# Transposed keys laid out by residue, and cached values loaded four rows to a partition, in a hybrid attention and GLA step

## The chip, the cores and the metric

One core of one Trainium2 chip runs the whole step. The metric is device time in microseconds (us), the median of three runs.

## What is computed

One layer of a hybrid decoder, for a prompt of 2048 positions and for eight samples of eight new positions each, which have 2048 cached keys and values per head. A normed input is projected; eight heads of 64 attend in three dilated windows, and the three results are mixed by their softmax denominators:

```python
DILATED = ((128, 1), (512, 4), (2048, 16))      # (window, dilation)
n_keys = window // dil + 1
...
s = jnp.einsum('brnqhd,brnkhd->brnqhk', qr, kk) * (hd ** -0.5)    # prompt: by residue modulo dil,
s = jnp.where(valid[None, None, :, :, None, :], s, -jnp.inf)      # blocks of 128 and the one before
...
idx = W + jnp.arange(T)[:, None] - dil * jnp.arange(n_keys)[None, :]   # sample: gathered from the cache
kg, vg = k_buf[:, idx], v_buf[:, idx]
```

Beside it a gated linear attention (GLA) of four heads runs in chunks. Both results are gated, concatenated, multiplied with `w_out` (1024 x 1024) and added to the input. Softmax sums over the keys of a window, so the order in which the keys of a block stand does not matter, as long as mask and values stand in the same order.

## The kernel before

Matrix products that need float32 accuracy are split into float16 parts: a projection of 128 rows is 8 x 3 matmuls, a score of 128 queries is two matmuls (the two orders of the key's high and low half). A cost-driven scheduler places the instructions on each engine; the Python code gives it generators that are woven in proportion to their steps. SP issues every DMA, in order. The stages, by first and last matmul in the trace:

- from 0 to 462 us, q, k and v are projected for 16 tiles of 128 rows (`project`, L1120). Each tile's keys and queries are stored in float16 to `kp_d` and `qp_d`, its values to `vp_d`, and come back transposed by DMA: `keys` (L838) fills `kk`, `queries` (L848) fills `qq`. `kk` holds, for each head, two groups of 512 positions (`m % 2`), each in the order of positions.
- from 113 to 625 us the branches 1 and 2 of the prompt's attention run between the projections. `unit(m, pp, br, x)` (L858) is 128 queries of four heads: for branch 1 the block x of 128 positions of group m, for branch 2 the residue x modulo 4 of group m. `attend` (L395) does it in four steps: `qk` (scores, L408, then minimum, mask and exp at L416 and L419), `tr` (transposes, L426, split into two float16 parts), `pv` (values, L441). The moving operand of L408 is a slice of `kk`: for branch 1 contiguous positions, for branch 2 every fourth position. The values of a unit are loaded 128 rows at a time (L883).
- on POOL and DVE the sample's scores against the cached keys run beside it (`sample_scores`, L985, `dot`, L978).
- branch 3 (L931) follows from 625 to 803 us, then the GLA with the projections g, vb and gb, to 1142 us.
- from 1142 us to the end, the output: `combine(t)` (L1501) loads the three branches and gates of tile t and mixes them, mostly on DVE and POOL; `turned` (L1447) transposes the mix (tm, L1453); `finish` (L1474) multiplies it with `w_out` in 48 matmuls of 512 columns (Y, L1488). The sample's attention is woven in: `sample_pair` (L1651) takes two samples at a time, four times. Its `values` (L1735) multiplies probabilities with cached values (L1737): four matmuls, each using 32 of the array's 128 columns. Each of the 13 blocks of cached values of a sample is a load of 128 rows x 512 numbers (256 KB, L1763), with 8 buffers. The last tile's output waits for the sample's attention and the sample's own output (Y_s).

```python
keys:    SP.dma_start_transpose(kk[:, :, m % 2, P * a : P * a + P], kp_d[r0 : r0 + P, :])
branch 2: of = lambda k: k[:, :, slice(x, 512, 4)]          # in scores, L906
values:  v = ssk.tile([P, 512], F32, ..., tag="sv", bufs=8)
         SP.dma_start(v[:], of(cv[2 * bp + bb]))
```

## Time and profile before

| | |
|---|---|
| three runs | 1419.62, 1424.39, 1426.09 us |
| median | 1424.39 us |
| span of the profiled execution | 1424.9 us |
| PE busy | 1285.0 us, 90% of the span |
| DVE, ACT, POOL busy | 1018.0, 843.7, 621.9 us |
| DMA | 281.57 MB on one queue, 67.1% of the time of 16 engines |
| HBM | 183.19 MB read, 75.24 MB written |

The profiled execution's span is the time from the first to the last instruction of the program; it lies 0.5 us above the median of the runs, inside their spread of 6.5 us, so nothing else has to be added to it. A row of the grouped view names source line, engine, operation, tiles and shape, count, then busy time, mean duration of one in ns, and idle time before them. A matmul's duration is the time through the array, longer than the time until the next one can start, which the timeline shows. PE is the matmul itself, PEld its weight load.

### The profile page before, as it was taken

Reading aid. Unit: us, or ns where it says so; the run is one execution under the profiler, and the core shown is the slowest. Engines: PE = TensorE matmul, PEld = TensorE weight load, DVE = VectorE, ACT = ScalarE, POOL = GpSimd, SP = SyncE. Lnnn points to the kernel's source line nnn. Section 1 sums busy time; section 2 is a strip of 40 time slices with the busy share of each in tenths; the row PEclk is TensorE's granted clock in tenths of the full one; section 3 lists DMA queues with packets and bytes.
Section 4 is the critical chain, followed back from the end, with each engine's and each line's share of the span. In section 5 each row is a group of like instructions: output and inputs, shape, how many; then the busy total and the mean of one; then the engine's idle time right before and its main releaser. Section 6 shows DMA issues by size and latency. Waiting matters only on the chain.

```text
span 1424.9 us, 26506 instructions
## 1 busy us (share of the span) xinstructions
PE 1285.0 (90%) x8942; PEld 743.6 (52%) x8942; DVE 1018.0 (71%) x2459; ACT 843.7 (59%) x2259; POOL 621.9 (44%) x564
## 2 busy tenths in 40 slices
PE   5989999889898898996889999889999989999997
PEld 2434555455455554664667666666555434444343
DVE  6797697789798967666775357898877797773222
ACT  6466787667377775875677665777876542221120
POOL 0144355566577455554421486556551264340000
PEclk9999999999999899997999999999999999999998
DMA  8469756678966797888976444242235759998661
GB/s 297 156 188 255 192 161 150 182 203 215 240 165 173 208 288 239 260 217 228 234 190 179 149 123 116 87 153 91 88 119 176 267 179 344 359 316 267 221 215 63
DMA packets 246874, 283.27 MB, mean 199 GB/s; under 512 B 117889, under 2 KB 148690, under 8 KB 246738
## 3 DMA queue, kind: packets, MB, share of 16 engines
q1 hardware_dynamic: 246738, 281.57, 67.1%
q8 instruction: 71, 1.16, 0.4%
q14 instruction: 65, 0.53, 0.1%
HBM read 183.19 MB, written 75.24 MB: 181 GB/s over the span
## 4 chain that ended last, share of the span: by engine, by line
PE 35%; DVE 25%; DMA 16%; ACT 11%; issue 7%; POOL 4%; SPq 2%; DVEq 0%; POOLq 0%; ACTq 0%
PE Y L1488 7%; PE acc_g L1120 3%; PE acc_vb L1120 3%; PE acc_k L1120 3%; DMA k<-in_cache_k_win 2%; POOL pr L980 2%; PE s L408 2%; PE OS L1737 2%; PE acc_qkb L1120 2%; ACT p L419 2%; DMA o_d<-o 2%; DMA oc<-o_d 2%; DVE p L416 2%; PE acc_v L1120 2%; DMA T_q<-qp_d 2%
## 5 line engine op out<-in xcount | busy, mean ns | idle before, releaser
L980 POOL TENSOR_TENSOR pr<-k,qb 128x512 f32<-128x512 f32 x128 | 171.8, 1342 | 184.9 <-DVE sck L981 113.9
L1120 PEld LDWEIGHTS <-hr 128*128 128x128 f16 x1824 | 177.7, 100 | 138.2 <-issue 17.6
L419 ACT ACTIVATE p<-p,o 128x256 f32<-128x256 f32 (+1 forms) x384 | 173.1, 453 | 86.0 <-DVE o L416 83.3
L1120 PEld LDWEIGHTS <-hl 128*128 128x128 f16 x1248 | 123.2, 100 | 146.6 <-issue 22.2
L1488 PE MATMUL Y<-w_o,mh 128*128 128x512 f16 x768 | 182.9, 385 | 8.3 <-ACT mh L1454 4.9
L416 DVE CUSTOM_DVE_ANT_0 p<-s,m3w,scl_s 128x256 f32<-128x256 f32 (+1 forms) x384 | 143.6, 419 | 39.0 <-DMA o_d<-o 20.3
L393 POOL TENSOR_TENSOR pt<-p,pt 128x512 f16<-128x512 f32 (+1 forms) x80 | 98.3, 1229 | 139.6 <-ACT pt L392 107.3
L441 PE MATMUL O<-v,pt 128*128 128x128 f16 x1200 | 116.1, 224 | 25.3 <-POOL pt L393 10.0
L426 PE MATMUL t<-ident,p 128*128 128x128 f32 x600 | 119.0, 289 | 14.5 <-ACT p L419 9.2
L1488 PEld LDWEIGHTS <-mh 128*128 128x128 f16 x768 | 72.5, 99 | 103.7 <-issue 25.2
L408 PE MATMUL s<-kk,qq 128*128 128x256 f16 (+1 forms) x512 | 105.7, 326 | 17.5 <-DVE o L416 12.4
L981 DVE TENSOR_REDUCE sck<-pr 128x8 f32<-128x512 f32 x128 | 87.0, 680 | 44.0 <-POOL pr L980 43.7
L441 PEld LDWEIGHTS <-pt 128*128 128x128 f16 x1200 | 86.6, 101 | 54.6 <-POOL pt L393 13.6
L1120 PE MATMUL acc_g<-w_g,hr 128*128 128x272 f16 (+1 forms) x768 | 103.3, 285 | 1.9 <-DVE so_g L677 1.0
L1120 PE MATMUL acc_v<-w_v,hl 128*128 128x512 f16 x384 | 99.5, 405 | 4.6 <-DMA hl<-ht 3.7
L426 PEld LDWEIGHTS t<-ident,p 128*128 128x128 f32 x600 | 73.5, 146 | 43.2 <-ACT p L419 26.4
L1120 PE MATMUL acc_q<-w_q,hl 128*128 128x512 f16 x384 | 92.0, 380 | 1.9 <-ACT zs_q L703 1.4
L1120 PE MATMUL acc_k<-w_k,hl 128*128 128x512 f16 x384 | 91.3, 382 | 2.5 <-ACT w_k L658 1.3
L1454 ACT ACTIVATE mh<-tm 128x1024 f16<-128x1024 f16 x32 | 31.7, 1019 | 104.1 <-PE tm L1453 97.7
L1120 PE MATMUL acc_gb<-w_gb,hr 128*128 128x512 f16 x384 | 90.0, 388 | 2.1 <-DVE so_gb L677 2.1
L1120 PE MATMUL acc_vb<-w_vb,hr 128*128 128x512 f16 x384 | 89.3, 379 | 1.6 <-DVE so_g L677 1.6
L212 ACT ACTIVATE E<-D_e 128x256 f32<-128x256 f32 (+1 forms) x168 | 67.7, 411 | 27.1 <-DVE ks L219 17.6
(533 smaller groups left out, 2628.1 us busy)
## 6 DMA issues: line engine op xcount, KB each, us to landing
k<-in_cache_k_win SPq DMA_DIRECT2D x104, 256.0 KB, 4.3
sv<-in_cache_v_win SPq DMA_DIRECT2D x104, 256.0 KB, 5.4
hr<-h_d SPq DMA_DIRECT2D x44, 512.0 KB, 4.1
qb<-q_d SPq DMA_DIRECT2D x64, 256.0 KB, 4.6
oc<-o_d SPq DMA_DIRECT2D x48, 264.0 KB, 5.8
o_d<-o SPq DMA_DIRECT2D x64, 132.0 KB, 3.9
x<-in_x_prompt SPq DMA_DIRECT2D x16, 512.0 KB, 5.8
h_d<-hl SPq DMA_DIRECT2D x16, 512.0 KB, 4.7
```

The source lines that it names most:

```text
L212: ACT.activation(E[rows, i, :n], D[rows, half], AF.Exp, scale=1.0 / 16.0)
L393: POOL.tensor_tensor(l, f, h, ALU.subtract)
L408: PE.matmul(s_ps[:, i * w : (i + 1) * w], q, k, start=(n == 0), stop=(n == len(prods) - 1),)
L416: DVE.tensor_tensor_reduce(s[:, sl], s_ps[:, sl], mask, neg, BIG, ALU.add, ALU.min, nmf(i))
L419: ACT.activation(s[:, sl], s[:, sl], AF.Exp, bias=nmf(i), scale=-1.0, accum_out=denf(i))
L426: PE.transpose(p_ps[:, i * P : (i + 1) * P], t["s"][:, i * P : (i + 1) * P], ident[:])
L441: PE.matmul(o_, t["pt"][:, c, (i * nb + b) * P : (i * nb + b + 1) * P], vf(i, b), start=(n == 0), stop=(n == 2 * nb - 1),)
L980: POOL.tensor_tensor(pr[:], kt, qt, ALU.mult)
L981: DVE.tensor_reduce(out, pr[:].rearrange("p (u k d) -> p u k d", u=2, k=4), AX.X, ALU.add)
L1120: PE.matmul(z, a_[:, k, :], w[:, p_, k, cols], start=(k == 0 and i == 0), stop=(k == KT - 1 and i == 2),)
L1454: ACT.activation(mhl[:, a], pt[:], AF.Copy)
L1488: PE.matmul(Y[:], a_[:, k, :], w_[:, part, k, :512], start=(i == 0), stop=(i == len(prods) - 1),)
```

## The change

It does four things.

1. `kk` holds each group of 512 positions by residue modulo 4: four runs of 128, each for one residue. A transposing DMA now takes 128 rows that stand four apart in `kp_d`. Branch 2 reads one contiguous run of 128 (or 256 over two groups). Branch 1 reads, for each block of 128 positions, four runs of 32 positions (64 bytes) out of the four residues; its keys stand in the order of residue, so it has a mask of its own (`m1w`), and its values are loaded in that order (`by4`).
2. The sample's cached values are loaded in four pieces instead of 13: one of 256 KB, and three of 1 MB in which a partition takes four neighbouring rows (8 KB). Buffers: six of 1 MB, two of 256 KB. A generator step multiplies sixteen matmuls (four rows x four quarters of the array) after a piece.
3. The sample's attention is announced to the weaving with 4 x 9 steps instead of 4 x 16.
4. Constants (`ident64`, `m3w`, `tabs`) move to pools with a shorter life, and `ident8` is gone.

```diff
+    def by4(ap):
+        return ap.rearrange("(c r) f -> r c f", r=4)
...
         def keys(m, a):
-            r0 = 512 * m + P * a
-            SP.dma_start_transpose(kk[:, :, m % 2, P * a : P * a + P], kp_d[r0 : r0 + P, :])
+            SP.dma_start_transpose(
+                kk[:, :, a, m % 2, :], by4(kp_d[512 * m : 512 * m + 512, :])[a]
+            )
...
-                SP.dma_start(vt[:], sel(vp_d[:, pp * 512 : (pp + 1) * 512]))
+                rows = sel(vp_d[:, pp * 512 : (pp + 1) * 512])
+                SP.dma_start(vt[:], by4(rows) if br == 1 else rows)
...
                 def scores(i, a=a):
+                    k = kk[:, 4 * pp + 2 * a + i]
+                    q = [qs_[m, pp][:, order_, 2 * a + i] for order_ in range(2)]
                     if br == 2:
-                        qs = slice(x, 512, 4)
-                        of = lambda k: k[:, :, qs] if nb == 2 else k[:, m % 2, qs]
+                        k = k[:, x] if nb == 2 else k[:, x, m % 2]
+                        q = [f[:, x::4] for f in q]
                     else:
...
+                        n0 = 4 * (m % 2) + x
+                        if x or m % 2 or nb == 1:
+                            of = slice(n0 - nb + 1, n0 + 1)
                         else:
+                            of = slice(0, 8, 7)
+                        k = k.rearrange("p r s (b c) -> p r (s b) c", c=32)
+                        k = k.rearrange("p r b c -> p b r c")[:, of]
...
-        kk = ap_.tile([P, NH, 2, 512], F16, name="kk", tag="kk", bufs=1)
+        kk = ap_.tile([P, NH, 4, 2, P], F16, name="kk", tag="kk", bufs=1)
...
-            for c in range(4):
-                src.append((
-                    lambda x, c=c: p2[:, x, 32 * c : 32 * c + 32],
-                    lambda v, c=c: v[W - 512 : W, :].rearrange("(j r) c -> r j c", r=4)[c],
+            pieces.append((
+                "b2", [lambda x, c=c: p2[:, x, 32 * c : 32 * c + 32] for c in range(4)],
+                lambda v: v[W - 512 : W, :].rearrange("(j r) c -> j r c", r=4),
+            ))
+            for t0 in (0, 4):
+                pieces.append((
+                    f"b3{t0}",
+                    [lambda x, t=t: p3[:, x, 32 * t : 32 * t + 32] for t in range(t0, t0 + 4)],
+                    lambda v, t0=t0: v.rearrange("(m r) c -> m r c", r=16)[:, t0 : t0 + 4],
                 ))
...
-                    v = ssk.tile([P, 512], F32, name=f"sv_{bp}_{bb}_{i}", tag="sv", bufs=8)
+                    v = ssk.tile(
+                        [P, n, 512], F32, name=f"sv_{bp}_{bb}_{nm_}", tag=f"sv{n}",
+                        bufs=2 if n == 1 else 6,
+                    )
                     SP.dma_start(v[:], of(cv[2 * bp + bb]))
                     vs_.append(v)
-                held.append((ps, vs_, i + 1))
-                if i % 2 == 0:
-                    while held:
-                        values(*held.pop(0))
+                for j, p_ in enumerate(ps):
+                    step += 1
+                    values(p_, [v[:, j] for v in vs_], step)
+                if n > 1:
                     yield
...
-        weave(out, [sample_attention(), 4 * 16])
+        weave(out, [sample_attention(), 4 * 9])
```

More of the change, by code (lines that the diff above doesn't have):

```diff
@@ L105, in tile_hymba @@
     nw = const("nw", [P, KT], A["norm_w"][0].rearrange("(k p) -> p k", p=P))
-    ident8 = cp.tile([P, P], F32, name="ident8")
-    DVE.tensor_scalar(ident8[:], ident[:], 0.125, None, ALU.mult)
-    ident64 = cp.tile([P, 64], F32, name="ident64")
-    for r0 in (0, 64):
-        DVE.tensor_copy(ident64[r0 : r0 + 64], ident8[r0 : r0 + 64, r0 : r0 + 64])
     ident16 = cp.tile([P, P], F16, name="ident16")
@@ L373, in tile_hymba, with const1 @@
         vp = c_att.enter_context(tc.tile_pool(name="vp", bufs=11))
[L375 to L376 removed]
+        def const1(name, shape, src, dt=F32, pool=kp):
+            t = pool.tile(shape, dt, name=name, bufs=1)
             SP.dma_start(t[:], src)
@@ L1025, in tile_hymba @@
         gnw = const1("gnw", [P, P], A["gla_norm_w"].to_broadcast([P, P]))
-        m3w = const1("m3w", [P, 384], A["c_m3"])
+        m3w = const1("m3w", [P, 384], A["c_m3"], pool=ap_)
+        m1w = ap_.tile([P, 384], F32, name="m1w", bufs=1)
+        by_c, by_r = "p (b c r) -> p b r c", "p (b r c) -> p b r c"
+        DVE.tensor_scalar(
+            m1w.rearrange(by_r, r=4, c=32), m3w.rearrange(by_c, r=4, c=32),
+            1e-10, None, ALU.mult,
+        )
         DVE.tensor_scalar(m3w[:], m3w[:], 1e-10, None, ALU.mult)
-        masks12 = (m3w[:, 0:256], m3w[:, 128:384])
+        masks12 = [(w[:, 0:256], w[:, 128:384]) for w in (m1w, m3w)]
         m3 = m3w[:, 128:256]
-        tabs = kp.tile([P, 2, 2, 64], F32, name="tabs")
+        tabs = ap_.tile([P, 2, 2, 64], F32, name="tabs", bufs=1)
         scl = {n_: kp.tile([P, 1], F32, name=f"scl_{n_}") for n_ in "qks"}
@@ L1243, in tile_hymba @@
         Sbd = []
-        st = {"wgu": wgu, "E": [], "ks": [], "qbd": []}
+        ident64 = gst.tile([P, 64], F32, name="ident64")
+        for r0 in (0, 64):
+            DVE.tensor_scalar(
+                ident64[r0 : r0 + 64], ident[r0 : r0 + 64, r0 : r0 + 64], 0.125, None, ALU.mult
+            )
+        st = {"wgu": wgu, "ident64": ident64, "E": [], "ks": [], "qbd": []}
         for i in range(2):
```

37 lines of the change are left out of this document (13 added, 24 removed).

## The prediction

> **What bounds the kernel now.** I read the page's head first, then the busy time by window for the two stages that the change touches: the prompt's attention (113 to 625 us) and the output with the sample's attention (1166 us to the end).
>
> ```profile
> span 1424.9 us, 26506 instructions
> PE 1285.0 (90%) x8942; PEld 743.6 (52%) x8942; DVE 1018.0 (71%) x2459; ACT 843.7 (59%) x2259; POOL 621.9 (44%) x564
> ...
> core 0: us, PE busy (x) PEld busy (x) DVE busy (x) ACT busy (x) POOL busy (x), PEclk, DMA share, GB/s
> 113.00:625.00 512.00, 469.54 (x3096) 280.38 (x3095) 406.95 (x970) 358.03 (x1012) 287.86 (x218) 0.97 0.76 209
> 1166.00:1425.00 259.00, 241.70 (x1611) 107.33 (x1609) 127.80 (x263) 51.84 (x81) 55.20 (x44) 0.98 0.75 254
> 1170.00:1300.00 130.00, 123.35 (x846) 57.54 (x844) 91.88 (x192) 31.47 (x50) 51.51 (x40) 0.99 0.94 329
> ```
>
> PE is the busiest engine in both. The reader should see two more things: DVE is at 407 of 512 us in the first stage, and the DMA engines are at 0.94 in the first half of the second. Next I asked what the little PE idle time of the first stage (42 us) waits for, and whether SP is held in the second.
>
> ```profile
> PE s L408 <- DVE o L416: 12.4, 12, 2.3
> PE O L441 <- POOL pt L393: 8.1, 11, 2.4
> PE s L408 <- DMA kk<-kp_d: 5.0, 2, 3.9
> ...
> SPq L1763 <- PE OS L1737: 47.7, 23, 8.2
> ```
>
> So the attention's own chain (scores, minimum, exp, split, values) holds PE now and then; keys do so twice. In the output stage SP stood 47.7 us before loads of cached values until PE had given a buffer back.
>
> **Part 1, keys by residue.** A matmul's duration is its time through the array; what counts is the distance to the next start, from the timeline. Four score matmuls of branch 2, then four of branch 1, all with 256 columns:
>
> ```profile
> 274.30 1.08 PE L408 MATMUL s<-kk,qq 128*128 128x256 f16 x4
> 275.20 1.05 PE L1120 MATMUL acc_v<-w_v,hl 128*128 128x512 f16 x4
> ...
> 308.19 0.60 PE L408 MATMUL s<-kk,qq 128*128 128x256 f16 x4
> 308.63 3.62 PE L1120 MATMUL acc_v<-w_v,hl 128*128 128x512 f16 x16
> ```
>
> Branch 2 takes 0.90/4 = 0.225 us each, branch 1 0.44/4 = 0.110 us. The shape is the same; the difference is that branch 2's keys stand 8 bytes apart and branch 1's are contiguous. [...]
>
> What limits the contiguous read of branch 2 is next. Its queries are still read at a stride by the weight load, and the groups by shape show that load in a stretch of branch 2 (260 to 294 us) and of branch 1 (296 to 327 us), and the 128-column scores of branch 2 (145 to 174 us) beside those of branch 3:
>
> ```profile
> L408 PEld LDWEIGHTS <-qq 128*128 128x128 f16 x28 | 3.1, 118 | 3.1 <-issue 1.6
> L408 PEld LDWEIGHTS <-qq 128*128 128x128 f16 x28 | 2.6, 97 | 1.4 <-issue 0.7
> ...
> L408 PE MATMUL s<-kk,qq 128*128 128x128 f16 x31 | 5.2, 292 | 0.0
> L408 PE MATMUL s<-T_k,T_q 128*128 128x128 f16 x256 | 24.8, 231 | 0.3 <-DVE o L416 0.3
> ```
>
> If the strided weight load cannot be repeated faster than every 0.118 us, the 192 matmuls of 256 columns (three groups x 64) save 192 x (0.225 - 0.118) = 20.5 us, and the 64 of the first group little; if it hides altogether, 192 x 0.115 + 64 x 0.061 = 26 us. I take 22 us of PE time.
>
> Branch 1 pays for it: 240 matmuls now read runs of 64 bytes. No row has that. Its neighbours are 0.110 us for contiguous reads and 0.225 us for 2-byte pieces at 8 bytes, so the cost lies between 0 and 240 x 0.115 = 28 us. I take 0: a run of 32 elements is much nearer to the first. It cannot be below 0, because 0.110 is 256 columns at the rate of the 512-column matmuls (0.216, below).
>
> How much of the 22 us reaches the span? In the order of the built program the first scores stand behind 447 projection matmuls instead of 338: `keys` now needs all four tiles of a group, so its transposes queue on SP behind the last store of the group, with value loads behind them. PE does 109 projection matmuls first (109 x 0.216 = 24 us), which wait for nothing, so PE loses nothing there. But the attention's DVE work then has 24 us less room (407 in 488 us, 83%), and the waits quoted above do not shrink with PE's work. I let 60% through: 13 us, between 0 and 26. The strided transposes themselves are covered: branch 3 transposes rows 16 apart in the same way.
>
> Branch 1's values are loaded with four runs of 32 rows instead of 128 rows. The nearest row:
>
> ```profile
> v<-vp_d SPq DMA_DIRECT2D x64, 128.0 KB, 3.9
> ```
>
> PE never waits for it now, since four buffers let it go ahead. Bounds: 0, and 10 us for 32 loads if a third of a microsecond of each shows; I take 2. [...]
>
> **Part 2, sixteen matmuls at a time.** Values matmuls use 32 columns of the array each, four side by side. Each appears as two passes in the trace, so four matmuls are eight rows. The timeline around two broken quads, around a long block, and the plain rate of Y:
>
> ```profile
> 1306.83 0.39 PE L1488 MATMUL Y<-w_o,mh 128*128 128x512 f16 x1
> 1307.15 0.63 PE L1737 MATMUL OS<-sv,P3x 128*32 128x256 f32 x6
> 1307.71 4.49 PE L1488 MATMUL Y<-w_o,mh 128*128 128x512 f16 x20
> ...
> 1369.73 0.38 PE L1488 MATMUL Y<-w_o,mh 128*128 128x512 f16 x1
> 1370.04 0.64 PE L1737 MATMUL OS<-vs_t,Pn 64*32 64x256 f32 x8
> 1372.47 1.90 PE L1488 MATMUL Y<-w_o,mh 128*128 128x512 f16 x8
> ...
> 1411.72 8.80 PE L1488 MATMUL Y<-w_o,mh 128*128 128x512 f16 x40
> ```
>
> Y alone: (8.80 - 0.38)/39 = 0.216 us. Before a values block PE loses 0.32 - 0.216 = 0.10 us, and three quarters of a quad take 0.56 us, as much as a whole one: 0.66 us per block of at most one quad. Five quads take 2.43 + 0.10 = 2.53 us. So a block costs 0.20 us plus 0.465 us per quad, and a quad cut in two costs 1.31 us. In the built order of before, the 56 quads are cut into 61 blocks by single Y matmuls (56 blocks of at most a quad, one of 1.0 us, four of five quads): 56 x 0.66 + 1.0 + 4 x 2.53 = 48 us. In the changed order they stand in 10 blocks: 10 x 0.20 + 56 x 0.465 = 28 us. PE is relieved of 20 us.
>
> But the order also shows where the time may go. The last block of values stood beside tiles 14 and 15 (its last start is 1394.4 us); now all four pairs are done before Y of tile 8.
>
> ```profile
> L1737 PE MATMUL OS<-sv,P3x x256: 379/379/404, 1217.3 to 1394.4; 128*32 128x256 f32 x128
> L1763 SPq DMA_DIRECT2D sv<-in_cache_v_win x104: 327/382/1975, 1169.9 to 1387.2; - x104
> sv<-in_cache_v_win SPq DMA_DIRECT2D x104, 256.0 KB, 5.4
> ...
> 1230.00:1240.00 10.00, 10.00 (x69) 4.01 (x68) 8.51 (x13) 3.10 (x4) 6.85 (x5) 1.00 1.04 390
> 1270.00:1280.00 10.00, 9.48 (x90) 4.49 (x88) 8.04 (x14) 2.16 (x3) 6.93 (x7) 1.00 0.69 210
> 1410.16 10.37 PE Y L1488 x48
> L1453 PE MATMUL tm<-ident,mt 128*128 128x128 f16 x256 | 22.2, 220 | 1.4 <-ACT mh L1454 1.3
> ```
>
> From the first load of cached values to the last, SP's changed order holds 51.6 MB: the 27.3 MB of values, and the branches, gates and inputs that stand between. That is a wall in front of tile 8. At the stage's mean (329 GB/s) it takes 157 us, at the best ten microseconds (390) 132 us. I take 370, since fewer and longer loads should keep the queue filled: 139 us. The last load lands and is multiplied in 6 us. Behind it stand eight tiles (8 x 10.37 = 83 us), five tiles' transposes (80 x 22.2/256 = 7 us), the sample's output (32 x 0.216 = 7 us) and the tail from the last Y (1411.72 + 8.80 = 1420.5) to 1424.9, 4.4 us: 101 us. The first load starts at 1170 us on before's clock; I see nothing that moves it. So this stage ends at 1170 + 139 + 6 + 101 = 1416, 9 us earlier: less than half of PE's 20 us, because DMA bounds its first half and PE its second. By the two other rates it ends at 1409 and 1434, so the term lies between -16 and +9.
>
> **Parts 3 and 4** cost nothing by themselves: 4 x 9 steps is what makes the order above, and `ident64` and `m1w` are one or two DVE instructions, at GLA's start and 60 us ahead of the first mask.
>
> **Sum.** 1425 - 13 + 2 - 9 = 1405 us, against the profiled execution's own 1424.9 us, which is 0.5 us above the median of the runs, so the same number holds for the median.
>
> **Rivals.**
> - Both parts go through: the weight load hides, SP never stands still, 390 GB/s. 1425 - 26 - 16 = 1383 us. For it, PE at 92% in both stages; against it, DVE and DMA close behind. Chance 0.13.
> - The attention's chain replaces PE as the bound, and part 1 brings nothing: 1425 + 2 - 9 = 1418 us, around the line between faster and same. For it, the waits on L416 and L393 and the later start. Chance 0.16.
> - Slower, by one mechanism: SP stands before a load of cached values until PE has freed one of six 1 MB buffers, the branch loads behind it wait too, and the wall of 51.6 MB moves at 300 GB/s or less (single windows show 210, and the 47.7 us of SP's waiting show that it happens). At 300: 172 us, so 1170 + 172 + 6 + 101 - 11 = 1438 us. It decides below about 310 GB/s; against it, each 1 MB buffer holds what four did. Chance 0.14.
> - The wall at 329 GB/s takes part 1's gain back: 1434 - 11 = 1423 us. Chance 0.10.
> - Runs of 64 bytes cost half of their bound (14 us): 1419 us. Chance 0.04.
> - The change doesn't do what it says, because contiguous keys read no faster, the distance being set by the strided queries: 1418 us. Chance 0.03; the 0.118 us of the weight load speaks against it. [...]
>
> **How the numbers follow.** The forecast itself has 0.40. About 0.5% (7 us) is what a measurement of this kernel can tell from no change. Faster: 0.40 + 0.13, half of the three cases around 1418 (0.11) and a little of the 1423 case: 0.65. Slower: 0.15. Same: 0.20. The range reaches from 1380 (both parts in full) to 1436, leaving out most of the slower case; the forecast's own range is 1392 to 1418.
>
> **What would show it.** Right: 128x256 scores of branch 2 at 0.11 to 0.12 us in the timeline; values in rows of 32 or more, no single Y between them; PE waiting for DMA `sv` before tile 8 and for nothing after it; DMA near idle in the last 90 us. Wrong: scores of branch 1 above 0.12 us; the first stage as long as before though its PE time fell; last values landing later than 1330 us; a wait for `v` that was not there.

## The result, and the profile after

The changed kernel takes 1433.56 us (median; 1429.29 to 1435.01) beside 1425.16 us of the kernel before (six runs of each): ratio 1.0054, 95% interval 1.0033 to 1.0076. It is slower by half a per cent; 1405 us and "faster" had been forecast. The profiled execution took 1429.29 us; its span, 1427.5 us, is 1.8 us less. Every run's time lies some 2 us above its span, so the two are not the same measure. Ratios use fast runs alone; that leaves out one run, of 3892 us, of the kernel called *changed, spread* below.

First the page's head, and the busy time by window: the prompt's attention by the clock of before, the same stage by its own first and last score, and the output.

```profile
span 1427.5 us, 26392 instructions
PE 1253.2 (88%) x8942; PEld 746.4 (52%) x8942; DVE 1019.9 (71%) x2459; ACT 844.1 (59%) x2259; POOL 622.2 (44%) x564
```

```profile
113.00:625.00 512.00, 446.94 (x3031) 270.81 (x3028) 390.81 (x941) 348.83 (x981) 275.29 (x212) 0.96 0.76 206
137.00:638.00 501.00, 437.22 (x3031) 269.72 (x3031) 385.29 (x945) 346.63 (x987) 276.62 (x213) 0.96 0.75 204
1166.00:1425.00 259.00, 231.55 (x1647) 113.94 (x1644) 129.92 (x277) 54.34 (x85) 56.89 (x43) 0.95 0.69 257
1170.00:1300.00 130.00, 114.71 (x954) 57.97 (x951) 85.64 (x194) 34.70 (x58) 42.23 (x33) 0.92 0.98 373
```

PE was busy for 32 us less over the span (1285.0 to 1253.2), and the span grew by 2.6. In the stretch from 113 to 625 us PE works 22.6 us less, and DVE 16 us less too: less was done by 625 us (3031 matmuls for 3096), not the same in less time. Attention now runs from 137 to 638 us. In its own stretch PE sat idle for 512 - 469.5 = 42.5 us before and for 501 - 437.2 = 63.8 us now.

The timeline shows whether the read became cheap: four score matmuls of branch 2 (at 293.78, 256 columns), then four of branch 1 (at 322.31), each followed by the next group.

```profile
293.78 0.60 PE L405 MATMUL s<-kk,qq 128*128 128x256 f16 x4
294.22 0.94 PE L438 MATMUL O<-v,pt 128*128 128x128 f16 x14
...
322.31 0.60 PE L405 MATMUL s<-kk,qq 128*128 128x256 f16 x4
322.75 2.97 PE L1126 MATMUL acc_k<-w_k,hl 128*128 128x512 f16 x13
```

In the first group of positions branch 2 has 128 columns. Such scores before, then after:

```profile
151.52 1.10 PE L408 MATMUL s<-kk,qq 128*128 128x128 f16 x8
152.45 4.50 PE L1120 MATMUL acc_v<-w_v,hl 128*128 128x512 f16 x20
```

```profile
160.13 0.39 PE L405 MATMUL s<-kk,qq 128*128 128x128 f16 x4
160.36 0.59 PE L1126 MATMUL acc_v<-w_v,hl 128*128 128x512 f16 x2
```

The groups by shape give the weight loads of these scores (count, busy time and mean ns of one, idle time before), and the waits tell PE's idle time from 137 to 640 us (total, times, longest):

```profile
L405 PEld LDWEIGHTS <-qq 128*128 128x128 f16 x380 | 40.1, 109 | 24.3 <-issue 17.0
```

```profile
PE s L405 <- DVE o L413: 14.1, 11, 3.2
PE O L438 <- POOL pt L390: 13.7, 17, 1.9
PE O L438 <- DVE pt L386: 12.9, 9, 4.2
PE t L423 <- ACT p L416: 8.1, 9, 3.9
PE s L405 <- DMA kk<-kp_d: 3.7, 2, 3.3
```

The same two waits for DVE's part of the split and for exp before (113 to 625 us):

```profile
PE O L441 <- DVE pt L389: 5.2, 6, 2.2
PE t L426 <- ACT p L419: 1.5, 5, 0.3
```

ACT's wait for the row minima, before and after, in the same two windows:

```profile
ACT p L419 <- DVE o L416: 66.9, 46, 4.6
```

```profile
ACT p L416 <- DVE o L413: 94.9, 55, 5.1
```

Both branches take 0.44/4 = 0.11 us for a matmul: branch 2 fell from 0.225 us, branch 1 with its runs of 64 bytes pays nothing. The 128-column scores fell from 0.93/8 = 0.116 us to 0.23/4 = 0.058, so the weight loads keep up there too: their mean of 0.109 us is the time that one takes, not the distance between two. But PE waits 13.7 us for POOL's part of the split where it waited 8.1, and 12.9 us for DVE's where it waited 5.2.

In the output stage the values now stand in long blocks, as the timeline shows for the last pair; then the loads of the cached values (shortest, median and longest issue, first and last start), the stretch between those starts by window, and the last 90 us:

```profile
1311.57 0.64 PE L1748 MATMUL OS<-sv_w,P 128*32 128x256 f32 x8
1312.02 1.91 PE L1748 MATMUL OS<-sv_b,P2x 128*32 128x256 f32 x32
1313.75 3.64 PE L1748 MATMUL OS<-sv_b,P3x 128*32 128x256 f32 x64
```

```profile
L1779 SPq DMA_DIRECT2D sv_b<-in_cache_v_win x24: 327/348/709, 1175.0 to 1301.6; - x24
L1779 SPq DMA_DIRECT2D sv_w<-in_cache_v_win x8: 332/379/1020, 1173.8 to 1285.3; - x8
```

```profile
1173.80:1301.60 127.80, 115.54 (x956) 58.52 (x957) 83.40 (x189) 33.01 (x56) 40.59 (x32) 0.93 0.99 378
1330.00:1420.00 90.00, 88.82 (x475) 42.44 (x474) 20.99 (x28) 15.33 (x17) 0.51 (x1) 1.00 0.26 90
```

The wall was there, and after 1330 us DMA is at 0.26, as foreseen. It moved at 378 GB/s, where 370 had been taken.

The prediction did not look at one thing in these rows, the granted clock (PEclk). In the traces of before and of the changed kernel it stands at 1.00 or at 0.50, with stretches at 0.50 of 3.4 to 20.5 us. Thirteen matmuls of Y in the changed kernel at 0.50, then 31 at 1.00:

```profile
1322.50:1329.00 6.50, 5.46 (x13) 1.87 (x13) 5.01 (x13) 0.22 (x1) 2.55 (x2) 0.50 0.34 113
1331.00:1337.50 6.50, 6.50 (x31) 2.91 (x30) 1.41 (x2) 0.60 (x1) 0.00 (x0) 1.00 0.20 74
```

They take 0.42 us each, then 0.21. The mean granted clock was 0.951 to 0.957 in the six runs of the changed kernel, and 0.964 to 0.976 in all runs of the kernel before beside which the experiments were measured. What makes it drop, no run separates.

### The profile page after: what moved, and what is told of

Same layout as the page of the kernel before. It is cut to its first block, busy times and chain, and to the rows that moved or that the text cites. A ratio compares the mean times of both kernels' runs of the same rounds, so it can differ in the third digit from the quotient of the medians.

```text
span 1427.5 us, 26392 instructions
## 1 busy us (share of the span) xinstructions
PE 1253.2 (88%) x8942; PEld 746.4 (52%) x8942; DVE 1019.9 (71%) x2459; ACT 844.1 (59%) x2259; POOL 622.2 (44%) x564
## 4 chain that ended last, share of the span: by engine, by line
DVE 29%; PE 25%; DMA 16%; issue 13%; ACT 10%; POOL 6%; SPq 2%; POOLq 0%; DVEq 0%; ACTq 0%
PE Y L1499 6%; DVE p L413 3%; DMA k<-in_cache_k_win 3%; POOL pr L980 3%; DMA o_d<-o 3%; PE acc_vb L1126 2%; PE acc_g L1126 2%; DMA oc<-o_d 2%; PE acc_v L1126 2%; ACT p L416 2%; PE acc_k L1126 2%; DVE qbd L217 2%; PE acc_qkb L1126 1%; PE s L405 1%; DMA T_q<-qp_d 1%
## 5 line engine op out<-in xcount | busy, mean ns | idle before, releaser
L1499 PE MATMUL Y<-w_o,mh 128*128 128x512 f16 x768 | 177.6, 390 | 12.8 <-DVE xr L1506 9.4
L390 POOL TENSOR_TENSOR pt<-p,pt 128x512 f16<-128x512 f32 (+1 forms) x80 | 93.1, 1164 | 134.7 <-ACT pt L389 103.1
L413 DVE CUSTOM_DVE_ANT_0 p<-s,m3w,scl_s 128x128 f32<-128x128 f32 (+1 forms) x256 | 88.5, 395 | 28.5 <-DMA o_d<-o 24.5
L405 PE MATMUL s<-kk,qq 128*128 128x256 f16 (+1 forms) x512 | 80.9, 279 | 18.2 <-DVE o L413 14.1
L1126 PE MATMUL acc_vb<-w_vb,hr 128*128 128x512 f16 x384 | 90.6, 379 | 0.8 <-DVE so_g L674 0.8
L1547 POOL TENSOR_TENSOR tc<-oc,w 128x512 f32<-128x512 f32 x32 | 46.2, 1464 | 91.5 <-DVE w L1539 90.2
```

Of the source, the lines that this page charges most:

```text
L390: POOL.tensor_tensor(l, f, h, ALU.subtract)
L405: PE.matmul(s_ps[:, i * w : (i + 1) * w], q, k, start=(n == 0), stop=(n == len(prods) - 1),)
L413: DVE.tensor_tensor_reduce(s[:, sl], s_ps[:, sl], mask, neg, BIG, ALU.add, ALU.min, nmf(i))
L1126: PE.matmul(z, a_[:, k, :], w[:, p_, k, cols], start=(k == 0 and i == 0), stop=(k == KT - 1 and i == 2),)
L1499: PE.matmul(Y[:], a_[:, k, :], w_[:, part, k, :512], start=(i == 0), stop=(i == len(prods) - 1),)
L1547: eng.tensor_tensor(t_[:], oc[:, g, :, 0:64], w[:, g].unsqueeze(2).to_broadcast([P, NH, HD]), ALU.mult,)
```

## The experiments

The stages of every kernel are read from its trace by the same marks, in us: first score of the prompt, last score of branches 1 and 2, last score of branch 3, last matmul of projection g, first and last Y. The ratio is to the kernel before. The last three columns are of PE up to branch 3's last score: busy, idle, and how much of the busy time fell into half clock; half of that is counted as lost (0.42 us for 0.21, above). By then every kernel has run nearly the same matmuls (4639 to 4693, in the two with another rate 4603 and 4563). Before itself is in two rows, since single profiled executions of one and the same prompt part differ by a few us: "before", "constants" and the two values kernels have one order on PE there, and so have "changed", "changed, spread" and "layout only", of which the first and the last stand 6.7 us apart at branch 3's end.

```
                         first s  last s  last s(3)  last g  first Y  last Y   ratio      busy   idle   half
before                     113.0   624.9    787.1     992.6   1148.2   1420.1   1        696.3   90.8   52.6
constants only             112.1   622.6    784.3     989.6   1143.3   1419.1   1.0002   693.5   90.8   43.7
changed                    137.3   638.4    797.2    1001.1   1156.0   1422.7   1.0054   682.2  115.0   69.5
values only                112.8   624.4    785.2     990.5   1146.6   1408.2   0.9938   697.1   88.1   55.0
layout only                140.4   643.7    803.9    1006.1   1161.2   1439.4   1.0146   680.3  123.6   65.0
late keys                  131.9   616.9    777.8    1014.2   1145.8   1421.2   1.0062   687.1   90.7   48.4
cheap read                 110.1   606.6    775.1     966.8   1136.2   1410.2   0.9944   675.9   99.2   51.8
cheap read, late keys      132.7   605.6    767.1     969.7   1126.1   1389.9   0.9779   663.7  103.3   37.5
four tiles                 136.1   604.6    765.6     978.7   1122.4   1405.2   0.9925   670.6   95.0   51.7
four tiles, late           136.8   618.2    784.9     997.7   1152.4   1424.5   1.0075   671.8  113.1   49.1
four tiles, group 0 late   136.4   622.1    785.2    1008.7   1153.5   1418.8   1.0002   678.1  107.2   64.3
changed, values in order   137.9   621.6    794.0     996.5   1160.7   1426.9   1.0030   681.6  112.4   57.7
  and natural key loads    137.6   620.3    788.5    1001.4   1158.5   1422.5   1.0018   670.6  117.9   51.3
changed, keys first        138.1   631.1    796.5    1006.4   1161.8   1426.1   1.0085   675.6  120.9   50.0
changed, early group 0     112.0   632.8    788.3     989.6   1148.7   1413.8   0.9965   679.7  108.6   72.2
changed, spread            139.4   640.8    800.2    1004.0   1159.4   1411.8   0.9993   685.4  114.8   75.2
changed, both repairs      110.7   631.6    785.7     987.0   1142.5   1398.7   0.9891   676.5  109.1   62.3
values and spread          113.3   625.4    785.4     990.8   1146.1   1398.3   0.9858   692.9   92.5   43.9
rate 0.70, before          111.5   615.7    787.7    1030.0   1162.1   1436.8   1.0092   681.1  106.6   43.9
rate 0.70, changed         139.5   621.4    784.7    1034.0   1171.2   1432.3   1.0103   659.4  125.3   50.8
```

**Which part costs.** Four kernels of one chip. The theory: attention starts late and loses that time; the values part gains.

*Constants only* (`ident64`, `m3w` and `tabs` as in the change, nothing else).

> The kernel before with only the constants moved (ident64 made in the gated stage, the mask and the rotary tables in another pool). TensorE's order is the one of before. Every theory: no change, 1425 us within 4, first prompt score at 113 us within 2. Anything beyond that would say that pool places alone move the time by as much as the whole change did.

Measured 1421.88 us beside 1422.44: 1.0002 (0.9985 to 1.0019). Part 4 costs nothing that can be measured.

*Values only* (the constants, and parts 2 to 4 of the diff, on the layout of before).

> The kernel before with the constants moved and the new values loads and blocks of the sample, without the residue layout of the keys. Theory L (the late start of attention costs the time, the values part gains): the prompt stage as before, first score at 113 us, the output stage shorter by what it gained in the changed kernel, 5 us: 1420 us (1415 to 1423). Rival W (the output stage gains nothing by itself and only took up what came late): 1425 within 3.

1414.67 us, 0.9938 (0.9920 to 0.9957): 8.8 us less by the ratio, where 5 had been expected.

*Layout only* (the changed kernel with `src` and `held` of the old values part).

> The changed kernel with the old values loads and blocks of the sample, so the residue layout alone. Theory L: first score at 137 us, the end of branch 3 some 9 us later than before (812 against 803), and with the old output stage all of that at the end: 1434 to 1439 us, slower than the changed kernel. Rival D (the prompt stage loses nothing by itself, the changed kernel's loss sits in the output stage's wall of loads): 1420 to 1427.

1442.09 us, 1.0146 (1.0117 to 1.0175), 20.8 us more by the ratio. The whole loss is in the key layout; 0.9938 x 1.0146 = 1.0083, a little above the changed kernel's 1.0054.

Where it is lost can be read from the kernels that share an order up to branch 3's last score, four with the old prompt part and three with the changed one. On average PE is busy for 695.0 us and idle for 90.6 in the four, busy for 682.6 and idle for 117.8 in the three: 12 us less busy, 27 us more waiting, 15 us later. And of the busy time 49 us fall into half clock in the four and 70 in the three, which takes back some 10 us of what the cheap read saves. The rows of constants only and of the changed kernel:

```profile
0.00:784.30 784.30, 693.46 (x4676) 419.20 (x4677) 604.11 (x1573) 534.26 (x1528) 366.72 (x296) 0.97 0.76 210
```

```profile
0.00:797.20 797.20, 682.19 (x4681) 418.48 (x4682) 602.15 (x1575) 536.72 (x1529) 360.69 (x296) 0.95 0.75 207
```

*Late keys* (the layout of before):

```diff
-    for a in range(4):
-        keys(m, a)
+    with tc.issue_after(stored["k", 4 * m + 3].ins):   # the group's last store to kp_d
+        for a in range(4):
+            keys(m, a)
```

> The kernel before with its own layout of the keys, but the four transposed key loads of a group queued behind the store of the group's last key tile; the first score stands behind 496 projection matmuls instead of 410 (519 in the changed kernel). No read becomes cheaper. Theory L: attention starts some 20 us later and all of that but a few us is lost: first score 130 to 137 us, branch 3's end 815 to 825, 1436 to 1447 us. Rival (attention has room to catch up, and the changed kernel lost its time elsewhere, in the order of the loads or in the waits of the values): 1423 to 1430 in spite of a start as late.

1431.21 us, 1.0062 (1.0038 to 1.0085). The time lies between the two ranges, and the stages speak against theory L: attention started 20 us late and branch 3's last score still came 6.5 us earlier than with early keys (777.8, 784.3), with PE idle as long (90.7 us, 90.8). What is lost is lost afterwards: projection g ends at 1014 us, 25 later. So the theory as stated fell: a late start alone does not delay the prompt part.

**Does the cheap read bring anything by itself?** Two kernels leave only the cheaper read, one with early keys and one with late ones. In the first of them the key blocks are ready a tile at a time, which true residues are not.

```diff
-    of = lambda k: k[:, :, qs] if nb == 2 else k[:, m % 2, qs]
+    ks = slice(P * x, P * x + P)
+    of = lambda k: k[:, :, ks] if nb == 2 else k[:, m % 2, ks]
```

> The kernel before with the constants moved, where branch 2 reads 128 neighbouring keys in place of every fourth, so its keys are other ones than the branch wants; no load, layout or mask changes. It leaves only the cheaper read (22 us of TensorE time by the start-to-start of 0.109 against 0.230 us). Theory C (the rate of a unit is set by minimum, exp and the splitting on DVE, ACT and POOL; TensorE's freed time turns into waits for p and pt): 1417 to 1423 us, PE's waits for pt and p in the prompt stage up by 10 us or more. Theory P (TensorE time passes through, the loss comes from the rest of the change): 1400 to 1408.

1417.94 us, 0.9944 (0.9923 to 0.9965).

The second adds the hold of the late kernel, all four key loads of a group behind its last key store:

> [...] Theory C: as the late kernel without the cheap read, 1426 to 1434 us. Theory P: 22 us less than that, 1408 to 1415. [...]

1395.04 us, 0.9779 (0.9750 to 0.9808). At branch 3's last score the cheap read gains 9.2 us with early keys (784.3 to 775.1) and 10.7 with late ones (777.8 to 767.1): about half of what PE saves, in both; PE's idle time grows by 8 and 13 us. The first time lies in theory C's range, the second is 13 us below theory P's: what reaches the end is another matter, 8 us and 38 us (1.0062 to 0.9779). Over the whole kernel PE worked for 63 us at half clock in the second and for 84 in the late kernel, so 10 of the 38 us are clock.

**Is it the wait for four tiles, or the late issue of their loads?** A residue load needs all four tiles of a group stored, and each unit needs all four loads. The next kernel has the second without the first: loads tile by tile as before, but branch 1 reads four runs of 32 keys from four tiles, and branch 2 neighbouring keys.

```diff
+    of = lambda k: k[:, m % 2].rearrange("p (a b c) -> p b a c", b=4, c=32)[:, x - nb + 1 : x + 1]
```

> The kernel before with the constants moved, its key loads tile by tile and its values loads unchanged, but branch 2 reads neighbouring keys and branch 1 reads four runs of 32 keys, one from each tile: other keys than wanted, but the same shapes, runs and the same wait for four tiles as the changed kernel. TensorE's order has the first score behind 449 projection matmuls (447 in the changed kernel). Theory W4 (waiting for four tiles and starting behind 110 more projection matmuls costs what the layout costs): 1436 to 1444 as the layout alone. Theory Q (the cost is in the four residue loads on SP's queue, which can't be issued before the group's last key is stored, and in the order the scheduler makes around them): near the late, cheap kernel, 1395 to 1410.

1414.81 us, 0.9925 (0.9909 to 0.9941). The first score stands behind 449 projection matmuls and comes at 136 us, as in the changed kernel, and branch 3's last score at 765.6 us is 18.7 us earlier than with the constants alone. Theory W4 is out: starting late and waiting for four tiles does not by itself cost anything. The time is 5 us above theory Q's range. Now the same with the four loads of a group held as in the late kernel:

> The kernel with the changed kernel's read shapes on the old layout (branch 1 four runs of 32 from four tiles, branch 2 neighbouring keys: other keys than wanted), now also with the four key loads of a group held behind the group's last key store, as the residue loads must be. Without that hold it ran 0.9925 of before, branch 3's last scores at 766 us. If the late issue of the loads is the layout's cost: branch 3's scores end at 785 to 800, 1428 to 1442 us. If it is not: 762 to 775 and 1408 to 1420.

1436.27 us, 1.0075 (1.0056 to 1.0094): branch 3's last score at 784.9, the gain is gone. Both kernels have run the same number of matmuls by that score, to one; the rows without the hold and with it:

```profile
0.00:765.60 765.60, 670.65 (x4655) 414.04 (x4656) 593.57 (x1570) 533.84 (x1524) 364.04 (x296) 0.96 0.79 215
```

```profile
0.00:784.90 784.90, 671.83 (x4654) 412.10 (x4655) 596.68 (x1569) 533.69 (x1526) 364.29 (x296) 0.96 0.77 210
```

PE is as busy, and idle for 18 us more (95.0 and 113.1). And with the hold on the first group alone:

```diff
-    with tc.issue_after(stored["k", 4 * m + 3].ins):
+    with ExitStack() if m else tc.issue_after(stored["k", 3].ins):
```

> The read shapes of the changed kernel on the old layout (other keys than wanted), key loads held behind the group's last key store for the first group only, later groups' loads tile by tile. Without any hold 0.9925 of before, with all held 1.0075. If the first group's late loads are the cost: its 64 score blocks take 102 to 106 us again (91.5 without the hold), branch 3's last scores at 778 to 786, 1428 to 1438 us. If the later groups share it evenly: 770 to 776, 1416 to 1424.

1423.06 us, 1.0002 (0.9979 to 1.0024); branch 3's last score at 785.2, as with all groups held. By the time, though, the first group and the later ones share it evenly (0.9925, 1.0002, 1.0075), as the rival expected, and the equal marks are partly chance: PE was idle for 107 us here and 113 with all held, and worked for 64 us at half clock in place of 49. ACT's wait for the row minima in the first group's stretch, without a hold (136 to 231 us), with it on the first group, and on all (136 to 241 us):

```profile
ACT p L413 <- DVE o L410: 7.7, 8, 2.3
```

```profile
ACT p L413 <- DVE o L410: 18.6, 9, 4.1
```

```profile
ACT p L413 <- DVE o L410: 19.6, 10, 4.6
```

The issues of the key loads, without a hold and with all held (the last two numbers are the first and the last start):

```profile
L835 SPq DMA_TRANSPOSE kk<-kp_d x16: 1231/1279/2096, 102.0 to 486.4; - x16
```

```profile
L835 SPq DMA_TRANSPOSE kk<-kp_d x16: 1237/1480/2870, 125.9 to 497.5; - x16
```

The first score comes at the same time in all three (136.1, 136.4, 136.8), but the first group's scores take 91.5, 104.2 and 104.0 us, in the changed kernel 105.4. That is not all waiting: between the first and the last of them stand 215 projection matmuls without the hold and 242 with it, 27 x 0.216 = 5.8 us of work done earlier, and PE's own idle time among them grows by 3 us only. The 18 us build up over the whole stage: 2 at the first score, 6 at the second group's, 13 at the fourth's, 18 at the end of branch 3.

What the hold changes is the order that the scheduler writes: ahead of branch 2 in the second half of the first group stand 624 projection matmuls without the hold and 644 with it, ahead of the second group 708 and 721. The first key load is held by 24 us, and all four are issued before the first score either way. The hold does not always cost this: on the layout of before it left PE's idle time as it was (90.8 and 90.7 us), and with the cheap read alone it added 4 us (99.2, 103.3) and branch 3 still ended earlier. The other order is the only thing that I see to make the difference. No kernel kept the order and moved the loads, so this path is argued and not shown; shown is that, where branch 1 reads from four tiles, the kernel with the hold and the order that comes with it takes 1.5% longer.

**What of the layout is left?** From 784.9 us (four tiles, late) the changed kernel's 797.2 is 12 us away. Three things are left: values of branch 1 in four runs, key loads of every fourth row, the residue layout with its mask. The values first (`by4(rows) if br == 1 else rows` becomes `rows`):

> The changed kernel with the values of branch 1 loaded in the order of positions as before (16 completion updates each, as the other loads, not 5); its probabilities then meet other values than they should. In the changed kernel these loads landed 4.9 us after their issue against 3.7 before, but 31 of 32 were there more than 0.6 us before their first matmul. So if that slack is right: no change against the changed kernel, 1427 to 1435 us. [...]

1428.15 us, 1.0030 (1.0014 to 1.0045). Then also the residue layout filled by natural loads, held as before:

```diff
-    kk[:, :, a, m % 2, :], by4(kp_d[512 * m : 512 * m + 512, :])[a]
+    kk[:, :, a, m % 2, :], kp_d[512 * m + P * a : 512 * m + P * a + P, :]
```

> The changed kernel with branch 1's values in the order of positions and the residue layout filled by natural tile loads, held behind the group's last key store (other keys and values than wanted; layout, masks, shapes and TensorE's order as in the changed kernel but for some places: first score behind 447, last group behind 1286). If reading every fourth row makes the loads slow or disturbs other transfers: 10 to 25 us below the changed kernel, 1405 to 1420. If the order is what costs (it hardly differs): like the kernel with natural values alone, 1425 to 1432.

1428.32 us, 1.0018 (1.0002 to 1.0035). The branch 3 marks go 797.2, 794.0, 788.5, 784.9; each step is within the scatter of single profiles, and the two ratios' intervals overlap. Reading every fourth row costs nothing that can be measured. Of the 12 us between the first and the last mark PE is busy in 10 and idle in 2, and half clock took 10 us of work from the changed kernel that the other kept (69.5 and 49.1 us at half clock); 27 matmuls more stand ahead of the mark, too. By the time the rest of the layout is small too: the last kernel holds the values part, worth 0.9938, and 1.0018/0.9938 = 1.0080 beside 1.0075 with four tiles held late. The changed kernel gives 1.0054/0.9938 = 1.0117 in this way; layout only was measured at 1.0146, 4 us above, which stays open.

**Repairs.** One place in the changed trace looked like a plain loss: SP's queue issues two transposed loads of branch 3 ahead of the last key load of group 3, for which the group's first score waits until 521.6 us:

```profile
508.31 2.93 SPq L936 DMA_TRANSPOSE T_q<-qp_d  x1
511.28 3.66 SPq L938 DMA_TRANSPOSE T_k<-kp_d  x1
...
515.67 1.24 SPq L837 DMA_TRANSPOSE kk<-kp_d  x1
```

```diff
+    with tc.issue_after(last_key[0].ins):          # around T_q and T_k
         SP.dma_start_transpose(q[:, 0], by16(qp_d, r))
```

> The changed kernel with branch 3's first transposed loads held on SP's queue until the last key load of group 3 is issued. In the changed kernel that key load was issued at 515.7 us, behind two transposed loads of branch 3 (3.0 and 3.7 us on the queue), 8 us after the last score of group 2; the first score of group 3 came at 521.6. Theory Q: the gap between the two groups shrinks from 13.8 to 6 to 8 us, branch 3 ends 5 to 8 us earlier, 1422 to 1428 us. Rival (the gap is filled elsewhere, or the later loads of branch 3 cost the same): 1430 to 1435.

1436.79 us, 1.0085 (1.0062 to 1.0109). The gap did shrink, from 13.8 to 9.5 us, and the last score of branch 2 came 7 us earlier; branch 3 then took 165.4 us in place of 158.8 and almost all was given back. The time is above the rival's range too, and not faster: a stall removed there brought nothing.

The first group's early start, by a copy of its keys in the order of positions:

```diff
+    def keys_first(a):                              # group 1's place, until its keys come
+        SP.dma_start_transpose(kk[:, :, a, 1, :], kp_d[P * a : P * a + P, :])
+    if m == 0: k = k[:, x - nb + 1 : x + 1, 1]      # branch 1 of group 0
```

> The changed kernel, but branch 1 of the first group of positions reads a copy of the keys in the order of positions (kept where group 1's keys come later), with its values in order too; the residue copy of group 0 is loaded when its branch 2 begins. So the first unit waits for one tile of keys again: TensorE's order puts it behind 338 projection matmuls of 512 columns as in the kernel before (447 in the changed kernel). If the wait for four tiles at the start is what costs: first score at 113 us, branch 3's end by 795, 1403 to 1413 us (the values part gave 8.8 by itself, 22 us of TensorE time are saved). If what costs is the residue layout past the start (other order, TensorE arriving early and waiting for ACT, DVE and POOL): 1415 to 1428.

1420.35 us, 0.9965 (0.9950 to 0.9981), 0.9% below the changed kernel. Branch 3's last score at 788.3 us is 9 earlier than in the changed kernel, but still 3 later than with the layout of before (785.2), and the time is in the second range: the early start buys back the loss and not the gain. What in it does so is not separated; it also takes the wait for four tiles and the values in four runs off the first group, and the scheduler writes another order.

The loads of cached values spread behind the output's stores:

```diff
+    held = ystores[-1] if bp else None
-    SP.dma_start(v[:], of(cv[2 * bp + bb]))
+    with tc.issue_after(held.ins) if held else ExitStack():
+        SP.dma_start(v[:], of(cv[2 * bp + bb]))
```

> The changed kernel with the cached values of sample pairs 1 to 3 queued behind the latest store of an output tile, so that these 1 MB loads no longer stand in one row ahead of the loads of tile 8. Theory W (in the output stage TensorE waits for transfers that stand behind the 51.6 MB of cached values): Y_8 back from 1323 to below 1300, the output stage 5 to 15 us shorter, 1415 to 1427 us. Rival (TensorE's own work and the pairs' chain set the stage's length, the wall is filled anyway): no change, 1428 to 1435, or worse where the later loads now end last.

1424.40 us, 0.9993 (0.9968 to 1.0017). Y of tile 8 starts at 1292.9 us in place of 1323.5, and the stage from first to last Y takes 252.4 us in place of 266.7, as theory W expected. Both repairs together:

> The whole change with both repairs: the first group's branch 1 on keys in the order of positions, and the cached values spread behind the output stores. The first gave 0.9965 of before, the second took 0.6% from the changed kernel. If they add: 0.989 to 0.993, 1409 to 1415 us. If one takes the other's gain: 1418 to 1424. The values part with the spread alone, without the key layout, ran 0.9858: above that the key layout still costs.

1408.07 us, 0.9891 (0.9863 to 0.9918): they add. The spread on the values part alone, without the key layout:

> The kernel before with the constants moved, the new values loads and blocks, and these loads spread behind the output stores; keys, scores and the whole prompt part as before. The values part alone gave 0.9938, the spreading 0.9939 on the changed kernel. If the two add: 1402 to 1410 us (ratio 0.985 to 0.989). If the spreading only takes back what the late prompt part had cost: 1413 to 1417.

1404.33 us, 0.9858 (0.9831 to 0.9884). It adds here too, and it is the fastest kernel with the whole computation, though its interval overlaps that of both repairs: whether the repaired key layout still costs is open; it gains nothing. The same 130 us of the changed kernel without and with the spread, then of the values part without and with it:

```profile
1200.00:1330.00 130.00, 112.19 (x1003) 56.96 (x1001) 80.55 (x199) 30.66 (x55) 40.22 (x33) 0.93 0.95 359
```

```profile
1200.00:1330.00 130.00, 123.52 (x947) 60.98 (x946) 81.91 (x189) 30.16 (x51) 42.11 (x35) 1.00 0.89 325
```

```profile
1200.00:1330.00 130.00, 113.07 (x983) 56.92 (x980) 79.33 (x192) 28.43 (x53) 39.24 (x32) 0.92 0.94 351
```

```profile
1200.00:1330.00 130.00, 121.91 (x946) 59.25 (x944) 83.64 (x183) 28.76 (x47) 41.25 (x32) 0.99 0.85 307
```

With DMA at 0.95 and 0.94 PE works for 112 and 113 of 130 us, and the clock is at 0.93 and 0.92; with the loads spread it works for 124 and 122, at 1.00 and 0.99.

**How much does an order alone move?** Attention is drawn in at a fixed rate per projection step; no work changes with it.

```diff
-    rate = 0.62
+    rate = 0.70
```

> The kernel before with the rate 0.70; no work changed. First score of group 3 behind 1200 projection matmuls (1264 before). It measures what an order alone moves in the kernel before. If the rate of before was the right one for its prices and only became wrong with the change: 1425 to 1440; if orders scatter the time whatever the work: anything from 1405 to 1445, with stage lengths that do not follow the work.

1439.49 us, 1.0092 (1.0071 to 1.0112). It lies in both expected ranges and so does not decide between them.

> The changed kernel with attention drawn in at 0.70 in place of 0.62 per projection step; no work changed. TensorE's order puts the first score of group 3 behind 1207 projection matmuls (1313 in the changed kernel, 1264 in the one before), the first of branch 3 behind 1484 (1588, 1539). If the order is the cost: branch 3's scores end by 775 to 785, 1412 to 1422 us. If the order is not: 1430 to 1436; or worse, if TensorE now waits more for p and pt.

1440.08 us, 1.0103 (1.0083 to 1.0124). The time misses the order theory's range by 18 us. The draw brings branch 3's last score in the changed kernel to 784.7 us as that theory wanted, 12.5 us earlier, with 118 matmuls fewer done by then, and projection g then ends 33 us later. From branch 3's last score to the last g both kernels take 242 to 249 us where their originals take 204 to 206; the late keys took 236. Orders move single stages by more than the change is worth, and both kernels took 0.5 to 0.9% longer with the other rate.

## Why the prediction was wrong

- **The price of the read: right in kind, and a little low.** 0.225 us was to become 0.118 or less; it became 0.11, and the 128-column scores went from 0.116 to 0.058. The 0.118 us of the strided weight load was its duration and no bound on the distance: it hides altogether, and the prediction's own sum for that case is 26 us, where 22 was taken.
- **The runs of 64 bytes: right**, 0 of a possible 28 us.
- **The failed step: "PE loses nothing there ... I let 60% through: 13 us, between 0 and 26."** The forecast saw that the first scores would stand behind 447 projection matmuls and start 24 us later (they did: 113.0 to 137.3), and excluded a loss by the argument that these projections wait for nothing. Layout alone measured +20.8 us, where -11 was forecast for it. What failed is the share that PE's waits may take: the forecast let them eat 9 of 22 us, and they ate more than all of it. Up to branch 3's last score PE waits 27 us longer with the changed prompt part (90.6 to 117.8), above all for exp (1.5 to 8.1 us in the lists above) and for the split (8.1 to 13.7 on POOL, 5.2 to 12.9 on DVE). The cheap read alone, on the old layout, raises the waiting by 8 to 13 us and passes 9 to 11 us on to branch 3's end, which is near the 60%. The rest came when branch 1 read from four tiles and the key loads were held behind the group's last store: 18 us more waiting and 1.5% of the time with the same read shapes. Which of the hold's effects does it is not shown; the order that the scheduler writes is the candidate.
- **A term that the sum does not have** is the granted clock. The changed prompt part runs 70 us of PE's work at half clock and the old one 49, a loss of some 10 us by branch 3's last score that no line of the prediction looked at.
- **The bound of the term** was wrong with it. A gain "between 0 and 26" held only for an order that stays; orders with no other work lengthened a single stage by 37 to 45 us.
- **The values of branch 1: right in size.** I took 2 us, bounds 0 and 10; values in order took the ratio from 1.0054 to 1.0030, some 3 us, with intervals that overlap. The third of a microsecond a load behind the bound was an estimate that no run had shown. The trace of the changed kernel shows 5 completion updates for each of these 32 loads where the other loads have 16 (32 x 11 = 352 fewer), and they land a median of 4.9 us after issue, against 3.7 before. How the 5 come about is not shown.
- **The output stage: right.** -9 us forecast, -8.8 measured with the values part alone. In that kernel PE was busy for 21 us less over the span (1286.1 to 1264.9; 20 forecast), the loads moved at 389 GB/s (370 taken), Y of tile 8 began at 1310.4 us (1315) and the span ended at 1413.0 (1416). In the changed kernel, behind the late prompt part, it was 12 us from the last load's issue to the block of its values (1301.6 to 1313.75) and 22 us to Y of tile 8, where 6 us and a few transposes had been allowed.
- **The rivals.** The slower rival, a wall at 300 GB/s or less, did not happen; slower came from the other part. The rival of the attention's chain (1418 us) had the right place: PE's waits for the split grew (8.1 to 13.7 and 5.2 to 12.9 us), and ACT's for the minima (66.9 to 94.9). It had no loss in it either.
- **The signs to look for.** Scores at 0.11 us, long values blocks and an idle DMA at the end came as written. A wait for `v` that was not there came too, once, for 1.2 us. PE's waiting for the cached values did not: its longest waits there are for the output buffers (Y behind DVE, 9.4 us). The sign "first stage as long as before though its PE time fell" is the one that came nearest: 501 us for 512 with 32 us less of PE, and 24 us later.

## What to carry to other kernels

Here the time that PE saved was worth what its waits left of it (12 us less busy, 27 us more waiting): count the engine's idle time up to a mark where the same work is done, before and after, and not the busy time in a fixed window. This kernel's queues run in an order that a scheduler wrote, and a saving of 20 us on one engine was smaller than what another order moved (37 to 45 us in a single stage); a layout that can only be filled behind the last of several stores changes that order. Undo the parts one at a time before a cause is believed, and give the term a loss side. Look at the granted clock beside the busy time, since a matmul of 512 columns took 0.42 us at half clock in place of 0.21. With the 1 MB loads spread in place of one row, Y of tile 8 started at 1292.9 us in place of 1323.5; spreading them was worth as much as the whole values part had gained (9 and 11 us, beside 8.8).

## What was not expected of the hardware

- Scores whose moving operand stands in runs of 64 bytes took 0.11 us for 256 columns, the same as contiguous ones, and half of the 0.225 us for 2-byte pieces 8 bytes apart.
- Key loads that transpose every fourth row of 2 KB left the kernel's time as loads of neighbouring rows did (1.0030 and 1.0018, intervals overlapping).
- The 32 loads of 128 KB in four runs of 32 rows completed with 5 updates each in place of 16, and landed a median of 1.2 us later (4.9 us after issue, 3.7 before).
- One core drew 378 GB/s over 128 us with loads of 1 MB, and 389 over 122 us in the kernel with the values part alone; the best ten microseconds of that stage before had been 390.
- The granted clock of PE stood at 0.50 for stretches of 3.4 to 20.5 us, and thirteen matmuls of 512 columns in one of them followed each other every 0.42 us, in place of 0.21 at 1.00.
